# Hybrid encoder layer: norm weights as rows, three squares on GpSimd, and another order of loads and sums in the first stage

## The chip, the cores and the metric

The kernel runs on one core of one Trainium2 chip. The metric is device time in microseconds (us) of one execution. A kernel is run several times, and its median is given. Engines: PE is TensorE, PEld its weight loads, DVE is VectorE, ACT is ScalarE, POOL is GpSimd, SP is SyncE, which here issues transfers (DMA).

## The reference

One layer on 1024 tokens of 1024 values, in float32. The change touches only the beginning of the first feed-forward block:

```
def rms_norm(x, g):
    y = x * rsqrt(mean(x * x, axis=-1) + 1e-6)
    return y * g

h = h + 0.5 * (silu(u @ w_gate) * (u @ w_up)) @ w_down      # u = rms_norm(h, ffn1_norm), D_FF = 2816
u = rms_norm(h, mix_norm); z = u @ w_in                     # then two attention branches
h = h + (sigmoid(ga) * (ya @ w_branch_a) + sigmoid(gb) * (yb @ w_branch_b)) @ w_out
h = h + 0.5 * (silu(v @ w_gate2) * (v @ w_up2)) @ w_down2   # v = rms_norm(h, ffn2_norm)
return rms_norm(h, final_norm)
```

## The kernel before, in words

**Float32 from three products.** Every float32 operand is split in two: a high half, rounded to fp32r by ACT (a copy, or `Copy` with a scale), and a low half, the difference, by DVE (L308 and L311 for weights, L810 and L812 for X, L831 and L833 for blocks of the normed input). A product of a 128-row chunk is three matmuls with 512 columns: high by high (L145), high by low (L147), low by high (L149).

**Seven products.** `hidden` and `products` (L233) compute gate and up projections in two-by-two blocks by a Strassen-like scheme with seven products P1 to P7 for each pair of output tiles i; "P2.1.0" in the tables is product P2 of pair 1, half 0 (gate; half 1 is up). Each has four chunks of three matmuls and one "mm" in the table issues one chunk.

**The input.** The host gives x twice: as rows of tokens (`x`, read into `toks`), and transposed (`xt`): 512 tokens by 128 features a tile. The tiles x:0 to x:3 hold the first half of the tokens: x:2 and x:3 (n = 1) are the features 512 to 1023, chunks X.0 to X.3 (X.0 and X.1 lie in x:2, X.2 and X.3 in x:3), and x:0 and x:1 (n = 0) the others. One norm factor is needed for each token, a sum over all features, so over all four tiles.

**The first stage** (`first_stage`, L734) is written out by hand, under a schedule that keeps the order as written on each engine. `LOADS` (L690) is the order of SP's transfers: x:t the transposed tiles, w:i.m weights of pair i, half m (512 KB; "w:0.1.1" is a part of 256 KB of it), k:t tiles of tokens, h:m second halves of weights. `load_early` (L274) and `fetch` (L284) issue the weights. `TABLE` (L694) is the order of all other work; each token is replayed by `do` (L774) on its own engine:

- `hi:X.c`, `lo:X.c`: halves of x times the norm weight (a scalar for each partition from the tile n1c), without the factor of the token. The P2 products use them raw: the factor is multiplied in afterwards.
- `square:n.c` (L777, ACT): the squares of one 128 x 512 chunk, scaled by 1/D. `add:k` (L780, DVE): sums of two such tiles, six in all; add:1 needs squares 1.0 and 1.1, add:2 square 1.2, add:3 square 1.3, add:4 square 0.0, and so on.
- `sum:0`, `sum:1` (L786, PE): each is four matmuls with the tile of squares as the weights and a column of ones, which gives four columns of means, tokens on partitions. `eps` (L790, DVE), `pow` (L793, POOL): the power -0.5. `spread` (L798, PE): four transposes that lay the factors out along the free axis on all partitions, in a PSUM bank. `keep` (L805, ACT): a copy of it into SBUF. `stat:t` (L801, ACT): sums of squares of the second half's tokens, from `toks`.
- `y:nh.c` (L817, DVE): x times weight times factor, in place; y:11 (n = 0) reads the factor in PSUM, behind `keep` in the order, y:21 (n = 1) reads the copy. `hi`/`lo:B11.c`: its halves, the right operand of the P1 products.
- `hi`/`lo:P2.0.0` and the like: halves of the weights. `mm`, `x`: one chunk of a product; the work behind a finished product.

Ahead of the table, the norm weights come as 128 partitions of 8 values by a transfer on ACT's queue (L739), an ACT instruction with `Silu` (L740) has its table loaded early, and `keep_busy(28)` (L727) runs 28 transposes of the identity on PE, so that it is at work while the first transfers are under way.

Behind the first stage `products.run` takes over, under the same queues; everything from there on is the same in both kernels.

## Time and profile before

| | before |
|---|---|
| runs | 1934.52, 1935.5, 1937.35 us; median 1935.5 us |
| profiled execution, span from first to last instruction | 1934.8 us (its time has no other record than this span) |
| ACT busy | 943.6 us, 49% of the span |
| POOL busy | 295.5 us, 15% |
| DMA, whole span | 298.70 MB, mean 154 GB/s |
| stretch 20 to 22 us: PE busy, granted clock, DMA | 2.00 of 2.00 us, 1.00, 408 GB/s |
| stretch 22 to 24 us: DVE busy | 2.00 of 2.00 us |

The profile is of one execution. Busy time is that of an engine's instructions; matmuls overlap, so a busy PE is not one at its peak, and the distance between the starts of matmuls says more. In a row of the timeline stand the start, the duration, the engine, the line, the operation with output and inputs, and in brackets how long the engine had been idle and what ended it. "SPq" and "ACTq" rows are the issue of a transfer, not the transfer.

### The profile page before, as it was taken

To read this page: it belongs to the slowest core of one execution; us is meant where nothing else is said; L and a number is where in the kernel's file an instruction comes from. 1 tells how busy PE (TensorE), PEld (TensorE's weight loads), DVE (VectorE), ACT (ScalarE), POOL (GpSimd) and SP (SyncE) were. 2 spreads that over 40 slices of the span, in tenths; PEclk is the share of its full clock that TensorE was granted. 3 is DMA by queue.
4 is the path that set the end of the run, shared out by engine and by line. 5 is a ranking of instruction groups with operands and counts; after the bars stand their busy time and mean duration, and the time that the engine had idled before them with its cause. 6 is when DMAs were issued, how large, how long until landed. Compare 5 with 4: busy or idle time off the path is not lost.

```text
span 1934.8 us, 25499 instructions
## 1 busy us (share of the span) xinstructions
PE 1922.2 (99%) x8956; PEld 1603.1 (83%) x8956; DVE 1437.1 (74%) x2560; ACT 943.6 (49%) x1827; POOL 295.5 (15%) x432
## 2 busy tenths in 40 slices
PE   9999999999999999999999999999999999999998
PEld 7888888888888888888888888878888888888886
DVE  7987765668957788678888857889676566569864
ACT  6532333344446543477877862365333333344453
POOL 0011110013300112211122231010111001005210
PEclk9999999999999999999999999999999999999999
DMA  6344323286234478553458576533423323493341
GB/s 261 100 167 163 129 104 128 86 289 225 88 109 137 159 223 250 185 163 104 116 134 195 184 242 210 169 140 133 147 87 109 126 87 109 140 355 104 112 144 61
DMA packets 151745, 298.70 MB, mean 154 GB/s; under 512 B 14912, under 2 KB 64448, under 8 KB 151616
## 3 DMA queue, kind: packets, MB, share of 16 engines
q1 hardware_dynamic: 123072, 210.53, 33.6%
q0 software_dynamic: 27824, 85.48, 13.3%
q8 instruction: 71, 1.16, 0.3%
q10 hardware_dynamic: 720, 1.05, 0.1%
q14 instruction: 58, 0.48, 0.1%
HBM read 210.50 MB, written 88.27 MB: 154 GB/s over the span
## 4 chain that ended last, share of the span: by engine, by line
PE 88%; issue 7%; POOL 1%; DMA 1%; DVE 1%; ACT 1%; POOLq 0%; SPq 0%; ACTq 0%; DVEq 0%
PE g L149 16%; PE g L147 16%; PE g L145 16%; PE d L149 11%; PE d L147 11%; PE d L145 11%; PE d L1299 2%; PE g L1313 1%; PE g L1318 1%; PE d L1278 1%; PE d L1279 1%; POOL zs_d L889 1%; PE d L138 1%; POOL z_d L891 1%; DMA zr_d<-xs 0%
## 5 line engine op out<-in xcount | busy, mean ns | idle before, releaser
L145 PE MATMUL g<-ar,ws 128*128 128x512 f32 x1128 | 423.1, 395 | 0.6 <-ACT fa L911 0.6
L147 PE MATMUL g<-ar,ws 128*128 128x512 f32 x1128 | 417.2, 390 | 0.9 <-DVE ar L94 0.5
L149 PE MATMUL g<-ar,ws 128*128 128x512 f32 x1128 | 416.1, 390 | 0.2 <-DVE ws L311 0.2
L145 PE MATMUL d<-ar,ws 128*128 128x512 f32 x736 | 282.4, 391 | 0.3 <-ACT ar L810 0.2
L147 PE MATMUL d<-ar,ws 128*128 128x512 f32 x736 | 281.9, 390 | 0.3 <-DVE ar L812 0.3
L149 PE MATMUL d<-ar,ws 128*128 128x512 f32 x736 | 281.6, 390 | 0.5 <-DVE ws L311 0.5
L147 PEld LDWEIGHTS g<-ar,ws 128*128 128x128 f32 x1128 | 211.8, 188 | 46.2 <-DVE ar L94 1.0
L149 PEld LDWEIGHTS g<-ar,ws 128*128 128x128 f32 x1128 | 211.7, 188 | 45.5 <-DVE ws L311 0.7
L145 PEld LDWEIGHTS g<-ar,ws 128*128 128x128 f32 x1128 | 206.4, 188 | 37.8 <-ACT fa L911 1.0
L311 DVE TENSOR_TENSOR ws<-raw,ws 128x512 fp32r<-128x512 f32 x204 | 139.6, 690 | 99.6 <-ACT ws L308 98.8
L308 ACT CAST ws<-raw 128x512 fp32r<-128x512 f32 x204 | 125.1, 620 | 140.6 <-PE g L149 64.4
L145 PEld LDWEIGHTS d<-ar,ws 128*128 128x128 f32 x736 | 138.3, 188 | 29.7 <-ACT ar L810 0.6
L147 PEld LDWEIGHTS d<-ar,ws 128*128 128x128 f32 x736 | 138.4, 188 | 29.6 <-DVE ar L812 0.6
L149 PEld LDWEIGHTS d<-ar,ws 128*128 128x128 f32 x736 | 138.4, 188 | 29.4 <-DVE ws L311 0.7
L93 ACT CAST ws<-raw 128x512 fp32r<-128x512 f32 (+1 forms) x121 | 81.0, 669 | 144.0 <-PE d L149 61.8
L94 DVE TENSOR_TENSOR ws<-raw,ws 128x512 fp32r<-128x512 f32 (+1 forms) x119 | 93.7, 789 | 59.8 <-ACT ws L93 59.3
L414 POOL DMA_DIRECT2D hid<-fx x91 | 49.3, 542 | 431.5 <-DVE fx L474 304.9
L93 ACT CAST ar<-raw 128x512 fp32r<-128x512 f32 (+1 forms) x83 | 56.0, 679 | 94.8 <-PE g L147 55.0
L94 DVE TENSOR_TENSOR ws<-ar,ws 128x512 fp32r<-128x512 f32 x114 | 98.3, 867 | 3.8 <-ACT ws L93 3.7
L145 PE MATMUL g<-ws,ws 128*128 128x512 f32 x232 | 91.0, 392 | 0.0
L149 PE MATMUL g<-ws,ws 128*128 128x512 f32 x232 | 90.5, 390 | 0.0
L147 PE MATMUL g<-ws,ws 128*128 128x512 f32 x232 | 90.3, 389 | 0.0
(313 smaller groups left out, 3607.4 us busy)
## 6 DMA issues: line engine op xcount, KB each, us to landing
raw<-hid SPq DMA_DIRECT2D x70, 512.0 KB
hid<-fx POOLq DMA_DIRECT2D x91, 256.0 KB, 2.4
ar<-in_ffn_w_down_dram SPq DMA_DIRECT2D x32, 512.0 KB
raw<-in_ffn_w_up_dram SPq DMA_DIRECT2D x31, 512.0 KB
raw<-in_ffn_w_gate_dram SPq DMA_DIRECT2D x27, 512.0 KB
raw<-in_w_in_dram SPq DMA_DIRECT2D x27, 512.0 KB
hid<-fa POOLq DMA_DIRECT2D x51, 256.0 KB, 2.7
ar<-zs_d POOLq DMA_DIRECT2D x48, 256.0 KB, 5.3
```

The source lines that it names most:

```text
L93: nc.scalar.copy(dst_hi, src)
L94: (eng or nc.vector).tensor_tensor(dst_lo, src, f32v(dst_hi), op=ALU.subtract)
L138: nc.tensor.transpose(pt[:, c * P:(c + 1) * P], xs[:, (half * 4 + c) * P:(half * 4 + c + 1) * P], ident)
L145: nc.tensor.matmul(b, lhs[0], r[0], start=first, stop=False, **kw)
L147: nc.tensor.matmul(b, lhs[0], r[1], start=False, stop=False, **kw)
L149: nc.tensor.matmul(b, lhs[1], r[0], start=False, stop=last, **kw)
L308: nc.scalar.copy(w[0][:, :512], a)
L311: nc.vector.tensor_tensor(w[0][:, 512:], a, f32v(w[0][:, :512]), op=ALU.subtract)
L414: nc.gpsimd.dma_start(hid[PRODUCTS.index(p), i], src)
L889: nc.gpsimd.dma_start(d[ch * P:(ch + 1) * P, cols], t)
L891: nc.gpsimd.dma_start(z_d[ch * P:(ch + 1) * P, cols], c)
L1299: nc.tensor.transpose(pt[:, i * P:(i + 1) * P], un["pr"][s][:, i * P:(i + 1) * P], ident)
```

## The change

- **Norm weights:** eight rows of 128 values, into a corner of the tile that also holds the ones. PE turns them (a transpose with eight rows), DVE copies the result to n1c. Of the 28 transposes of `keep_busy` 6 stay ahead of it and 10 behind. The `Silu` that loads ACT's table works on a corner of another small tile, which is set again afterwards.
- **Squares:** 1.2, 1.3 and 0.0 are a multiplication of the chunk by itself on GpSimd; the other five stay on ACT. The scale 1/D moves to `eps`.
- **Sums:** the column of ones is now 128 columns, so that each matmul of `sum` gives 128 equal columns, four of them a whole PSUM bank; `eps` reads one column of each.
- **Transfers:** w:1.0 and w:1.1 in two parts each, with the parts for P2 (w:1.0.1, w:1.1.1) early; w:0.1.1 ahead of x:3; w:0.0.0 and w:0.1.0 ahead of k:4. SP issues two more transfers.
- **Order:** P2.0.0 and P2.0.1 take turns on X.0 and X.1 before X.2 is used; three chunks of P2.1.0 stand ahead of the sums, its last and the first of P2.1.1 between the sums and the spread; y:11.0 stands right behind the spread, and `keep` comes later, behind all of y:11; halves of B11 alternate with y:11.

```diff
--- before.py
+++ after.py
@@ -275,7 +275,7 @@
 
             if i:
                 ahead[i, m] = r
-                fetch(r, i, m, 0)
+                fetch(r, i, m, 0, slice(0, NC8) if part is None else slice(4 * part, 4 * part + 4))
             else:
                 if (0, m, 0) not in raws:
                     raws[0, m, 0] = raw_slot()
@@ -688,16 +688,18 @@
 
 
     LOADS = """
-        x:2.0 w:0.0.1 x:2.1 x:3 w:0.1.1 x:0 x:1 w:1.0 k:4 w:0.0.0 w:1.1 k:6 w:0.1.0 x:5 k:7 k:5 x:4 x:6 w:2.1 w:2.0
+        x:2.0 w:0.0.1 x:2.1 w:0.1.1 x:3 w:1.0.1 x:0 x:1 w:1.1.1 w:0.0.0 w:0.1.0 k:4 w:1.0.0 w:1.1.0 k:6 x:5 k:7 k:5 x:4 x:6
+        w:2.1 w:2.0
         h:0 h:1 w:3.0 x:7 w:3.1 w:4.1 w:4.0
     """
     TABLE = """
-        hi:X.0 hi:P2.0.0 lo:X.0 square:1.0 lo:P2.0.0 hi:X.1 mm:P2.0.0 square:1.1 lo:X.1 hi:X.2 add:1 mm:P2.0.0 hi:X.3
-        lo:X.2 hi:P2.0.1 lo:X.3 mm:P2.0.0 square:1.2 lo:P2.0.1 square:1.3 mm:P2.0.0 add:2 square:0.0 mm:P2.0.1
-        square:0.1 add:3 mm:P2.0.1 square:0.2 add:4 mm:P2.0.1 square:0.3 add:5 mm:P2.0.1 hi:P2.1.0 add:6 sum:0
-        hi:P1.1.0 lo:P2.1.0 sum:1 stat:4 lo:P1.1.0 mm:P2.1.0 eps:0 hi:P1.0.0 pow:0 mm:P2.1.0 lo:P1.0.0 mm:P2.1.0
-        hi:P2.1.1 hi:P1.1.1 spread:0 lo:P2.1.1 mm:P2.1.0 keep:0 y:11.0 mm:P2.1.1 stat:6 y:11.1 mm:P2.1.1 y:11.2
-        hi:B11.0 mm:P2.1.1 y:11.3 hi:P1.0.1 mm:P2.1.1 lo:B11.0 hi:B11.1 hi:B11.2 lo:P1.0.1 mm:P1.0.0 hi:B11.3 lo:B11.1
+        hi:X.0 hi:P2.0.0 lo:X.0 lo:P2.0.0 hi:X.1 mm:P2.0.0 square:1.0 lo:X.1 hi:P2.0.1 mm:P2.0.0 square:1.1 lo:P2.0.1 hi:X.2
+        mm:P2.0.1 add:1 mm:P2.0.1 lo:X.2 hi:X.3 mm:P2.0.0 lo:X.3 square:1.2 mm:P2.0.1 square:1.3 add:2 mm:P2.0.0
+        hi:P2.1.0 add:3 mm:P2.0.1 square:0.0 lo:P2.1.0 square:0.1 add:4 mm:P2.1.0 square:0.2 add:5 mm:P2.1.0
+        square:0.3 mm:P2.1.0 add:6 sum:0 hi:P2.1.1 hi:P1.0.0 sum:1 lo:P2.1.1 hi:P1.0.1 lo:P1.0.0 eps:0 stat:4 pow:0
+        mm:P2.1.0 lo:P1.0.1 mm:P2.1.1 spread:0 hi:P1.1.0 y:11.0 mm:P2.1.1 y:11.1 hi:B11.0 mm:P2.1.1
+        lo:B11.0 hi:B11.1 mm:P2.1.1 y:11.2 lo:B11.1 hi:P1.1.1 y:11.3 lo:P1.1.0 hi:B11.2 stat:6
+        mm:P1.0.0 hi:B11.3 keep:0
         mm:P1.0.1 stat:7 lo:B11.2 mm:P1.0.0 lo:B11.3 mm:P1.0.1 stat:5 lo:P1.1.1 mm:P1.0.0 x:P2.0.1 mm:P1.0.1 x:P2.1.0
         mm:P1.0.0 y:21.2 mm:P1.0.1 y:21.3 hi:B21.2 mm:P1.1.0 y:21.0 hi:B21.3 mm:P1.1.0 lo:B21.2 hi:B21.0 mm:P1.1.0
         eps:1 hi:P1.2.1 lo:B21.0 pow:1 mm:P1.1.0 hi:P2.2.1 lo:P1.2.1 hi:P1.2.0 mm:P1.1.1 lo:P2.2.1 hi:P2.2.0 mm:P1.1.1
@@ -734,11 +736,12 @@
     def first_stage():
         load, _, _, _, pieces, (multiply, finish), hand_over, load_early = hg
         n1c = const.tile([P, NC8], F32, name="n1c")
-        ones = const.tile([P, 1], F32, name="ones")
+        ones = const.tile([P, 1152], F32, tag="gain", bufs=1, name="ones")
+        ones, n1r = ones[:, :P], ones[:NC8, P:2 * P]
         nc.gpsimd.memset(ones, 1.0)
-        nc.scalar.dma_start(n1c, n1)
-        nc.scalar.activation(ones, ones, AF.Silu)
-        nc.gpsimd.memset(ones, 1.0)
+        nc.scalar.dma_start(n1r, n1)
+        nc.scalar.activation(nhalf4[:, 3:4], nhalf4[:, 3:4], AF.Silu)
+        nc.gpsimd.memset(nhalf4, -0.5)
 
         toks, early = new_ar(4, F32), [new_ar(g, F32) for g in (5, 6)]
         for token in LOADS.split():
@@ -754,7 +757,7 @@
                 load(0, t, 1, 2 + t)
             else:
                 k = 2 * (t - 1) + a[1]
-                load_early(t, a[1], early[k // 4][:, k % 4] if t else None, a[-1])
+                load_early(t, a[1], early[k // 4][:, k % 4] if t else None, a[2] if len(a) > 2 else None)
         room = [xs4(), xs4()]
         sq = [room[k // 2][:, k % 2 * 512:k % 2 * 512 + 512] for k in range(4)]
 
@@ -774,7 +777,11 @@
         def do(op, a):
             if op == "square":
                 n, c = int(a[0]), int(a[1])
-                nc.scalar.activation(sq[place[4 * (1 - n) + c]], block(c, 0, n), AF.Square, scale=D ** -0.5)
+                q, b = sq[place[4 * (1 - n) + c]], block(c, 0, n)
+                if a[0] + a[1] in ("12", "13", "00"):
+                    nc.gpsimd.tensor_tensor(q, b, b, op=ALU.mult)
+                else:
+                    nc.scalar.activation(q, b, AF.Square)
             elif op == "add":
                 d, e = [sq[k] for k in sums[int(a[0])]]
                 nc.vector.tensor_tensor(d, d, e, op=ALU.add)
@@ -783,11 +790,12 @@
                 if i == 0:
                     mean.append(bank("g"))
                 for k in range(4):
-                    nc.tensor.matmul(mean[0][:, k:k + 1], sq[3 * i][:, k * P:(k + 1) * P], ones, start=i + k == 0, stop=i == 1,
-                                     skip_group_check=True)
+                    nc.tensor.matmul(mean[0][:, k * P:(k + 1) * P], sq[3 * i][:, k * P:(k + 1) * P], ones, start=i + k == 0,
+                                     stop=i == 1, skip_group_check=True)
             elif op == "eps":
                 i = int(a[0])
-                nc.vector.tensor_scalar(st[i][1], st[1][0] if i else mean[0][:, :4], EPS, None, op0=ALU.add)
+                ms = st[1][0] if i else mean[0].rearrange("p (k f) -> p k f", f=P)[:, :, 0]
+                nc.vector.tensor_scalar(st[i][1], ms, 1.0 if i else 1.0 / D, EPS, op0=ALU.mult, op1=ALU.add)
             elif op == "pow":
                 i = int(a[0])
                 nc.gpsimd.tensor_tensor(st[i][0], st[i][1], nhalf4, op=ALU.pow)
@@ -847,7 +855,11 @@
                         pc[q] = pieces(*q)
                     pc[q].pop(op)()
 
-        keep_busy(28)
+        keep_busy(6)
+        pt = bank("g")
+        nc.tensor.transpose(pt[:, :NC8], n1r, ident[:NC8, :NC8])
+        nc.vector.tensor_copy(n1c, pt[:, :NC8])
+        keep_busy(10)
         for token in TABLE.split():
             op, a = token.split(":")
             do(op, a.split("."))
@@ -1536,7 +1548,7 @@
     first, second = data["x"].reshape(2, 512, D)
     data["xt"] = np.concatenate([first.reshape(512, 2, 2, 2, P).transpose(1, 2, 4, 3, 0).reshape(4, P, D),
                                  second.reshape(512, 2, 4, P).transpose(2, 3, 1, 0).reshape(4, P, D)])
-    data["ffn1_norm"] = data["ffn1_norm"].reshape(NC8, P).T
+    data["ffn1_norm"] = data["ffn1_norm"].reshape(NC8, P)
     for name in ("ffn1_w_gate", "ffn1_w_up", "ffn2_w_gate", "ffn2_w_up"):
         data[name] = data[name].reshape(NC8, P, NF, P).transpose(2, 1, 0, 3)
     data = {name: data[name] for name in _INS}
```

## The prediction

> **What bounds the kernel now.** I read the page first: busy shares and the chain that ended last.
>
> ```profile
> span 1934.8 us, 25499 instructions
> ...
> PE 1922.2 (99%) x8956; PEld 1603.1 (83%) x8956; DVE 1437.1 (74%) x2560; ACT 943.6 (49%) x1827; POOL 295.5 (15%) x432
> ...
> PE 88%; issue 7%; POOL 1%; DMA 1%; DVE 1%; ACT 1%; POOLq 0%; SPq 0%; ACTq 0%; DVEq 0%
> ```
>
> TensorE bounds the kernel from end to end: 1922.2 of 1934.8 us, so it is idle for 12.6 us in all. The diff touches only the first 30 us. Built, the two programs differ in their first 79 (before) and 68 (after) PE instructions and agree in the 8870 behind them; the last 2527 on DVE, 1639 on ACT, 424 on POOL and 488 on SP agree in order too. So the question is how much earlier or later PE leaves the first stage; what it gains there it keeps as long as the later transfers allow.
>
> Next the timeline of the first 30 us. Columns: start, duration, engine, line, operation, and in brackets the idle time before it and what ended that. Here PE is not simply busy.
>
> ```profile
> 0.73 0.40 ACTq L739 DMA_DIRECT2D n1c<-in_ffn_norm_dram  x1
> ...
> 1.38 5.38 PE L732 MATMUL g<-ident 128*128 128x128 f32 x28 [1.38 <-POOL ident masks.py:199]
> ...
> 3.90 0.72 ACT L810 ACTIVATE ar<-fx,n1c 128x512 fp32r<-128x512 f32 x1 [1.24 <-DMA n1c<-in_ffn_norm_dram]
> ...
> 4.62 0.62 ACT L308 CAST ws<-raw 128x512 fp32r<-128x512 f32 x1
> ...
> 6.52 0.48 PE L145 MATMUL d<-ar,ws 128*128 128x512 f32 x1
> ...
> 7.57 0.33 SPq L752 DMA_DIRECT2D ar<-in_x_dram  x1
> ...
> 7.58 1.34 ACT L810 ACTIVATE ar<-fx,n1c 128x512 fp32r<-128x512 f32 x2 [0.68 <-DMA fx<-in_xt_dram]
> ...
> 7.76 0.40 PE L149 MATMUL d<-ar,ws 128*128 128x512 f32 x1
> ...
> 8.36 0.51 PE L145 MATMUL d<-ar,ws 128*128 128x512 f32 x1 [0.19 <-ACT ar L810]
> 8.57 0.33 SPq L285 DMA_DIRECT2D raw<-in_ffn_w_up_dram  x1
> ...
> 9.14 0.50 PE L147 MATMUL d<-ar,ws 128*128 128x512 f32 x1 [0.28 <-DVE ar L812]
> ...
> 10.40 0.39 PE L145 MATMUL d<-ar,ws 128*128 128x512 f32 x1
> ...
> 10.62 0.40 PE L147 MATMUL d<-ar,ws 128*128 128x512 f32 x1
> ...
> 12.90 0.39 PE L149 MATMUL d<-ar,ws 128*128 128x512 f32 x1
> ...
> 13.49 1.92 PE L786 MATMUL g<-ones,xs 128*128 128x1 f32 x16 [0.20 <-DVE xs L780]
> ...
> 15.27 0.48 PE L145 MATMUL d<-ar,ws 128*128 128x512 f32 x1
> ...
> 15.45 0.16 DVE L790 TENSOR_SCALAR st<-g 128x4 f32<-128x4 f32 x1 [0.29 <-PE g L786]
> ...
> 16.09 0.63 PE L145 MATMUL d<-ar,ws 128*128 128x512 f32 x1
> ...
> 18.65 0.96 PE L798 MATMUL g<-ident,st 128*128 128x128 f32 x4
> ...
> 19.36 0.48 PE L145 MATMUL d<-ar,ws 128*128 128x512 f32 x1
> ...
> 22.90 0.39 PE L145 MATMUL g<-ar,ws 128*128 128x512 f32 x1
> ...
> 23.65 0.50 PE L147 MATMUL g<-ar,ws 128*128 128x512 f32 x1 [0.36 <-DVE ar L833]
> ```
>
> The same timeline, PE alone, at the end of the stage:
>
> ```profile
> 29.00 0.39 PE L145 MATMUL g<-ar,ws 128*128 128x512 f32 x1
> ...
> 31.72 0.39 PE L145 MATMUL g<-ar,ws 128*128 128x512 f32 x1
> ```
>
> Twelve matmuls lie between 29.00 and 31.72, so one is issued each 0.227 us. From 6.52 to 29.00 there are 72 of them (six products of four chunks of three), 16.36 us at that pace in 22.48 us: **6.12 us are lost**. Where: before X.2 the starts are 7.76, 8.36, 9.14, and the three gaps about them cost 1.0; the sums lie between 12.90 and 15.27 and cost 2.14 (2.37 less 0.23); six matmuls from 16.09 to 18.65 take 2.56 instead of 1.36, 1.2 lost; the spread, 18.65 to 19.36, costs 0.7; the wait for B11's low half, 22.90 to 23.65, costs 0.6 with its restart. That is 5.7; some 0.4 I cannot place.
>
> The table by stretches says what the slow matmuls are (columns: busy time of PE, PEld, DVE, ACT, POOL; granted clock; DMA share; GB/s):
>
> ```profile
> 16.00:18.00 2.00, 2.00 (x6) 1.53 (x6) 1.13 (x2) 0.87 (x2) 0.79 (x1) 0.50 1.03 402
> ...
> 12.56:15.98 3.42, 3.22 (x23) 2.70 (x22) 2.81 (x6) 3.40 (x7) 0.22 (x1) 1.00 1.04 412
> ...
> 5.74:9.15 3.41, 2.94 (x17) 2.00 (x15) 2.44 (x5) 2.73 (x6) 0.00 (x0) 1.00 1.00 351
> ```
>
> From 16 us the granted clock is 0.50, just behind the stretch with 1.92 us of one-column sums. DMA is at its full share of 1.0, 402 to 412 GB/s: order of transfers is a matter of who waits, not of volume.
>
> **The change, part by part.** *Norm weights and warm-up.* Before, the high half of X.0 waited for n1c until 3.90 and the first weight half was cast by 5.24, but PE came out of its 28 transposes only at 6.52. After, 6 transposes, the turn of n1, a DVE copy (0.16 by L790's row) and 10 more. Twenty-eight took 5.38, 0.19 each, so 17 take 3.3 and end near 4.9 unless n1 is late. When eight rows land no row shows; the bounds are the end of their issue (1.1) and as late as before (3.9). Up to some 3.4 the weight half, cast by 5.24 as now, is the later one, and the first matmul comes at 5.3; at 3.9 eleven transposes follow, 0.2 each, and it comes at 6.2. I take 5.3, as fewer and longer rows should not be slower than many short ones: 1.2 earlier.
>
> *Order of transfers and of the first matmuls.* Both P2 products now take X.0 and X.1 first: twelve matmuls, 5.3 to 8.03 (9.0 at the late bound). But x:3 goes behind w:0.1.1. SP's issues at 7.57 and 8.57 each follow the landing of an older transfer, of x:3 and of w:0.1.1 as I read them; exchanged, x:3 lands at 8.57, 1.0 later. The high half of X.2 is then there at 9.3 and the 13th matmul starts at 9.36, against 10.40 before: 1.0 ahead, whatever the start was. PE has waited 1.33 for it, so the earlier first matmul is worth nothing by itself. The halves of w:1.0 and w:1.1 that P2.1 needs come some 3 us earlier; the two extra SP issues cost 0.33 each on a queue that waits anyway. Nothing there.
>
> *Three squares on GpSimd.* ACT is rid of three squares of 0.6 us. What they do to DVE is the disputed price. Far from here, GpSimd and DVE work side by side on such tiles (timeline of POOL and of DVE, then the groups of POOL):
>
> ```profile
> 454.91 6.69 POOL L563 TENSOR_TENSOR ar<-ar,ar 128x512 f32<-128x512 f32 x4 [19.72 <-DMA ar<-in_ffn_w_down_dram]
> ```
> ```profile
> 454.64 0.69 DVE L94 TENSOR_TENSOR ws<-raw,ws 128x512 fp32r<-128x512 f32 x1 [0.93 <-ACT ws L93]
> 455.25 1.78 DVE L94 TENSOR_TENSOR ws<-ar,ws 128x512 fp32r<-128x512 f32 x1
> 457.07 1.68 DVE L560 TENSOR_TENSOR ar<-ar,ar 128x512 f32<-128x512 f32 x1
> ```
> ```profile
> L94 POOL TENSOR_TENSOR ws<-raw,ws 128x512 fp32r<-128x512 f32 x2 | 2.5, 1292 | 14.6 <-ACT ws L93 14.6
> ```
>
> DVE's two-input operation takes 0.69 alone and 1.68 to 1.78 beside GpSimd, whose own takes 1.67 (6.69 for four) instead of 1.29: they take turns. Applied here: the first square starts with x:3 at 8.6 and ends at 9.85; X.2's low half on DVE (9.36) waits for it and ends at 10.40 instead of 10.1, so the 14th matmul starts at 10.44 (before 10.62). X.3's low half ends at 11.06; the second square, which had its turn in between, at 11.56; add:2 at 12.1; the third square at 13.3; add:3 at 13.8; and the low half of P2.1.0, queued behind add:3, at 14.44. PE has done 24 matmuls by 13.0 and stands before the third of P2.1.0 from 13.45 to 14.48: a new hole of 1.1 with its restart. Without turns that half is ready at 12.9 and there is no hole.
>
> *Sums with 128 columns.* PE instructions stay 16. The bounds are 0.1 each (as now) and 0.23 (a 512-column matmul, or a cold transpose): 1.7 to 3.6. The nearest row is the 128-column transposes of the same type, 0.19 mostly cold and half of it warm; I take 1.8 in all, with no wait, as P2.1.0 covers the adds: 0.35 less than before. The cold stretch behind them, 1.2, should go, since the array streams 128 columns where it had one.
>
> *The rest.* 1/D in the eps operation costs nothing (same instruction). Spread after the first chunk of P2.1.1: 0.44 warm and 0.15 of wait for the power, against 0.7. The y of B11 no longer stand behind the copy; B11's first low half comes 1.3 earlier, but PE is there earlier too and waits 0.65 in two places, as before.
>
> **Sum**, to the 73rd matmul: 5.3 + 16.36 + 1.33 + 0.86 (X.2's halves) + 1.1 + 1.8 + 0.6 + 0.65 = 28.0; with 0.3 for what I could not place, 28.3, against 29.00. That is **0.7 us earlier**, at most 0 if a later transfer holds PE. The profiled execution's span is 1934.8 and the runs have a median of 1935.5 (1934.52 to 1937.35); from between the two, 1935.1, less 0.7: 1934.4.
>
> **Rivals.** *Squares ride free.* If a square (one tile read twice) does not make DVE take turns, the 1.1 hole and 0.3 at X.2 go: 28.3 less 1.4, 2.1 us gained, about 1933.0. For it: no row has a GpSimd operation with one input twice. Against: in the rows above every such pair of operations took turns.
>
> *Slower: PE's clock drops in the new holes.* It decides at the granted clock from 16 us on. The stretch before that has a hole of 1.1 of 3.4 us; if it drops the clock as the one-column sums did, 16 sum instructions at 0.21 instead of 0.11 cost 1.7, within a slow stretch as long as before's (16.09 to 19.36). The end is 28.3 + 1.7 = 30.0, 1.0 later than before: 1936.1. For it: before, the clock fell behind a stretch whose PE idle time was 0.2 us, with less than half of it in 512-column matmuls. Against: behind 5.74 to 9.15, with 0.47 idle, it stayed at 1.00. The Trainium skill, "TensorE: Matmul & The Clock Gate", Part 1 (What's actually happening), says that the clock halves only after a whole idle window of about 3.4 us; by that rule this rival costs nothing. The trace does not bear it out: the 0.50 at 16 us follows no idle window.
>
> *It doesn't do what it says.* The x:3 wait eats the front and the rest is even: PE leaves where it left, 1935.1; this lies inside the forecast's own spread.
>
> **How the numbers follow.** The forecast with its even variant 0.55 (1933.7 to 1935.8), squares free 0.22, clock drop 0.17, unforeseen 0.06. The runs of before alone spread over 2.8 us, so I widen both ends: from 1931.9 (squares free, 1.1 below) to 1937.2 (clock drop and a high median). A measurement of this kernel tells about 0.2%, 3.9 us, from no change: faster than 1931.6 needs squares free and more, 0.11; slower than 1939.4 needs a cold clock in two stretches, 0.08; within 0.81.
>
> **What would show it.** In the changed kernel: first matmul near 5.3; 13th at 9.4 behind X.2; squares on POOL of 1.2 to 1.7 us with DVE's low halves and adds stretched to 1.1 to 1.7; a hole of 1 us in P2.1.0 at 13.5 to 14.5; granted clock 1.00 from 16 to 20; 73rd matmul near 28.3. Wrong if DVE's operations beside the squares take 0.7, if the clock is 0.50 anywhere behind 6 us, or if x:3 lands before 8.

## The result, and the profile after

The changed kernel has a median of 1939.28 us (13 runs, 1936.99 to 1942.19) against 1936.07 of the kernel before (13 runs, 1934.52 to 1938.03): a ratio of 1.0015 [1.0008, 1.0022], so it is **slower by 0.15%**, some 3 us. Forecast were 0.7 us gained and 1931.9 to 1937.2: the sign is wrong, and the time lies outside the range. The difference is less than the 0.2% that I took for what a measurement can tell; thirteen runs of each tell more. The execution profiled took 1939.36 us. First its page, the rows that answer to those of before.

```profile
span 1937.3 us, 25481 instructions
...
PE 1922.6 (99%) x8945; PEld 1601.0 (83%) x8945; DVE 1438.7 (74%) x2561; ACT 942.6 (49%) x1824; POOL 299.4 (15%) x435
...
q8 instruction: 70, 1.15, 0.2%
...
PE 87%; issue 8%; POOL 2%; DVE 1%; DMA 1%; ACT 1%; SPq 0%; POOLq 0%; ACTq 0%; DVEq 0%
```

PE is as busy as before (1922.6 us against 1922.2), but the span is 2.5 us longer: it is idle for more. Next the first 30 us of the changed kernel, all engines (start, duration, engine, line, operation, idle time before and what ended it), and PE alone at the end of the stage.

```profile
2.96 0.27 PE L860 MATMUL g<-ident,ones 8*128 8x8 f32 x1
...
5.45 0.80 PE L145 MATMUL d<-ar,ws 128*128 128x512 f32 x1
...
7.68 0.80 PE L145 MATMUL d<-ar,ws 128*128 128x512 f32 x1 [0.58 <-ACT ar L818]
...
9.41 1.33 ACT L818 ACTIVATE ar<-fx,n1c 128x512 fp32r<-128x512 f32 x2 [0.16 <-DMA fx<-in_xt_dram]
9.46 4.38 POOL L782 TENSOR_TENSOR xs<-fx 128x512 f32<-128x512 f32 x3 [6.46 <-DMA fx<-in_xt_dram]
9.48 0.63 PE L145 MATMUL d<-ar,ws 128*128 128x512 f32 x1
...
9.91 0.63 PE L147 MATMUL d<-ar,ws 128*128 128x512 f32 x1
...
10.17 2.77 DVE L820 SCALAR_TENSOR_TENSOR ar<-fx,n1c,ar 128x512 fp32r<-128x512 f32 x2
...
11.62 0.39 PE L145 MATMUL d<-ar,ws 128*128 128x512 f32 x1
...
12.86 2.32 DVE L787 TENSOR_TENSOR xs<-xs,xs 128x512 f32<-128x512 f32 x2
...
15.10 0.68 DVE L311 TENSOR_TENSOR ws<-ar,ws 128x512 fp32r<-128x512 f32 x1
...
15.84 0.50 PE L149 MATMUL d<-ar,ws 128*128 128x512 f32 x1 [0.86 <-DVE ws L311]
```
```profile
17.58 1.95 PE L793 MATMUL g<-ones,xs 128*128 128x128 f32 x16
19.28 0.48 PE L145 MATMUL d<-ar,ws 128*128 128x512 f32 x1
...
20.52 0.40 PE L149 MATMUL d<-ar,ws 128*128 128x512 f32 x1
21.27 0.65 PE L806 MATMUL g<-ident,st 128*128 128x128 f32 x4 [0.35 <-POOL st L801]
21.68 0.48 PE L145 MATMUL d<-ar,ws 128*128 128x512 f32 x1
...
29.91 0.39 PE L145 MATMUL g<-ar,ws 128*128 128x512 f32 x1
```

Three things are to be seen. The first matmul comes at 5.45, but up to 10.8 two matmuls are 0.43 apart (9.48, 9.91), not 0.23: PE runs at half speed. The three squares on POOL (4.38) stand beside two low halves on DVE (2.77) and two adds (2.32); behind them PE waits before 15.84 for the low half of P2.1.0. This chain on DVE begins behind X.2's high half, which ACT could start only when x:3 had landed, at 9.41; from 10.17 to 15.78 DVE has no pause. The sums take 1.70 (17.58 to 19.28), with no slow matmul behind them. The 73rd matmul starts at 29.91 instead of 29.00.

So the stage accounts for 0.9 us of the 2.5 by which the span grew. The other 1.6 lie **behind** it, where the forecast had nothing. Set beside those of before in order, the starts of PE's instructions show two places where it loses over half a microsecond. Here they are in the timeline of the changed kernel (PE, then all engines).

```profile
972.24 0.44 PE L1311 MATMUL d<-ident,fa 128*128 128x128 f32 x2 [0.34 <-DVE ws L94]
```
```profile
1088.25 2.39 POOL L94 TENSOR_TENSOR ar<-raw,ar 128x1024 fp32r<-128x1024 f32 x1 [1.76 <-ACT ar L93]
...
1088.28 2.78 DVE L1085 TENSOR_TENSOR fa<-raw,masks 128x384 f32<-128x384 f32 x1
...
1091.45 0.44 PE L1290 MATMUL d<-ar,ar 128*128 128x384 f32 x1 [1.08 <-DVE nmx L1295]
```

At 971 PE loses 0.74 us, at 1090 1.4; small gains and losses elsewhere come to −0.5. The diff touches neither place.

### The profile page after: what moved, and what is told of

The parts are those of the page before. It is cut to its first block, busy times and chain, and to the rows that moved or that the text cites. A ratio compares the mean times of both kernels' runs of the same rounds, so it can differ in the third digit from the quotient of the medians.

```text
span 1937.3 us, 25481 instructions
## 1 busy us (share of the span) xinstructions
PE 1922.6 (99%) x8945; PEld 1601.0 (83%) x8945; DVE 1438.7 (74%) x2561; ACT 942.6 (49%) x1824; POOL 299.4 (15%) x435
## 3 DMA queue, kind: packets, MB, share of 16 engines
q8 instruction: 70, 1.15, 0.2%
q10 hardware_dynamic: 592, 1.05, 0.1%
## 4 chain that ended last, share of the span: by engine, by line
PE 87%; issue 8%; POOL 2%; DVE 1%; DMA 1%; ACT 1%; SPq 0%; POOLq 0%; ACTq 0%; DVEq 0%
PE g L149 16%; PE g L147 16%; PE g L145 16%; PE d L149 11%; PE d L147 11%; PE d L145 11%; PE d L1311 2%; PE g L1330 1%; PE d L1290 1%; PE d L1291 1%; PE g L1325 1%; POOL zs_d L901 1%; PE d L138 1%; POOL z_d L903 1%; DMA fx<-in_xt_dram 0%
## 5 line engine op out<-in xcount | busy, mean ns | idle before, releaser
L145 PE MATMUL g<-ws,ws 128*128 128x512 f32 x232 | 91.0, 392 | 0.0
L1298 ACT ACTIVATE fa<-fa,nmx 128x385 f32<-128x385 f32 (+3 forms) x128 | 75.7, 592 | 31.1 <-DVE nmx L1295 30.3
L149 PE MATMUL g<-ws,ws 128*128 128x512 f32 x232 | 90.4, 390 | 0.0
```

The costliest lines, as they stand in the source:

```text
L145: nc.tensor.matmul(b, lhs[0], r[0], start=first, stop=False, **kw)
L149: nc.tensor.matmul(b, lhs[1], r[0], start=False, stop=last, **kw)
L1298: nc.scalar.activation(pr, pr, AF.Exp, scale=-1.0, bias=nmx[:, s:s + 1], accum_out=ssum[:, s:s + 1])
```

## The experiments

All runs in one table. "73rd" is the start of the 73rd matmul in the profiled execution; "behind" is what is left of the span from there, against the 1905.8 us (1934.8 less 29.00) of the kernel before in its first trace. Times are medians of 11 runs (13 in the first row), beside those of the kernel before measured together with them; ratios have 95% intervals. before_2, before_3 and after_2 are single executions. A profiled execution need not be typical: those of a_sq_act (1934.56) and b_16 (1935.34) are the fastest of their eleven.

| run | us | before | ratio | 73rd | behind |
|---|---|---|---|---|---|
| changed kernel | 1939.28 | 1936.07 | 1.0015 [1.0008, 1.0022] | 29.91 | +1.6 |
| after_2 (again) | 1942.11 | 1935.85 | | 29.11 | +5.4 |
| before_2, before_3 | 1935.61, 1935.63 | 1935.85 | | 28.99, 28.73 | −1.0, −0.6 |
| a_sq_act | 1937.22 | 1936.14 | 1.0006 [0.9997, 1.0015] | 27.15 | −0.2 |
| a_warm | 1937.28 | 1936.14 | 1.0005 [0.9996, 1.0014] | 28.62 | +1.1 |
| a_warm_sq | 1936.56 | 1935.89 | 1.0004 [0.9995, 1.0013] | 27.93 | −0.1 |
| a_late_spread | 1936.68 | 1935.85 | 1.0003 [0.9994, 1.0012] | 27.48 | +1.6 |
| a_loads_old | 1938.98 | 1936.14 | 1.0014 [1.0005, 1.0023] | 30.96 | +1.2 |
| a_sum1 | 1938.46 | 1936.14 | 1.0012 [1.0003, 1.0020] | 29.55 | +2.3 |
| a_pad | 1938.45 | 1936.42 | 1.0007 [0.9998, 1.0016] | 29.81 | +0.9 |
| a_sq_pad | 1937.58 | 1936.42 | 1.0004 [0.9995, 1.0013] | 28.85 | +1.8 |
| b_sq_pool | 1939.08 | 1935.89 | 1.0016 [1.0007, 1.0025] | 31.19 | −1.2 |
| b_front | 1937.18 | 1935.89 | 1.0006 [0.9997, 1.0015] | 27.76 | +1.4 |
| b_16 | 1937.84 | 1936.42 | 1.0008 [0.9999, 1.0017] | 27.70 | +0.1 |
| b_sum128 | 1935.44 | 1935.89 | 0.9999 [0.9990, 1.0008] | 27.56 | +0.1 |
| b_sum128_2 | 1936.35 | 1936.42 | 0.9999 [0.9991, 1.0008] | 27.99 | +0.8 |

A median's interval is about ±1.7 us wide, as wide as most of the steps. So the stage is read from the traces, and the medians only bear out the sum.

**Squares.** a_sq_act is the changed kernel with all squares on ACT; b_sq_pool is the kernel before with the three squares on GpSimd.

```diff
-                if a[0] + a[1] in ("12", "13", "00"):
+                if a[0] + a[1] in ():
```

> The changed kernel with all eight squares on ACT again; everything else as changed. Theory A (GpSimd's squares hold DVE up): in the changed kernel the low halves of X.2 and X.3 took 2.77 us for two and the low half of P2.1.0 was ready only at 15.8; without GpSimd's squares it is ready by 14.4, the hole before the 27th matmul (14.59 to 15.84) goes, and the first stage ends 1.0 us earlier than in the changed kernel (73rd matmul at 28.9 instead of 29.91). Theory B (the cold clock and the late transfers at the front are the loss): the 27th matmul moves by under 0.3 us and the stage ends where it did, 29.9. Theory C (what is lost is lost behind the first stage): the stage may gain, but the time stays near 1939.

In b_sq_pool the same branch, with 1/D moved to `eps`, is put into the kernel before:

```diff
-                nc.scalar.activation(sq[place[4 * (1 - n) + c]], block(c, 0, n), AF.Square, scale=D ** -0.5)
+                q, b = sq[place[4 * (1 - n) + c]], block(c, 0, n)
+                if a[0] + a[1] in ("12", "13", "00"):
+                    nc.gpsimd.tensor_tensor(q, b, b, op=ALU.mult)
+                else:
+                    nc.scalar.activation(q, b, AF.Square)
```

> The kernel before with one part of the change: squares 1.2, 1.3 and 0.0 on GpSimd. Theory A (GpSimd's squares hold DVE up): the two low halves of X.2 and X.3 take over 2 us instead of 1.41, the second operand of X.2 comes at 9.7 or later instead of 9.14, the sums start 0.5 to 1.5 us later than 13.49, and the stage ends 0.5 to 1.5 us later than 29.0. Rival (the squares ride free): DVE's times as before, stage end within 0.3 us.

Timelines of a_sq_act, and of after_2 (the changed kernel, in a trace in which x:3 landed at the same time as there), each with the 27th matmul as its last row:

```profile
8.61 1.34 ACT L818 ACTIVATE ar<-fx,n1c 128x512 fp32r<-128x512 f32 x2 [0.53 <-DMA fx<-in_xt_dram]
...
9.37 1.41 DVE L820 SCALAR_TENSOR_TENSOR ar<-fx,n1c,ar 128x512 fp32r<-128x512 f32 x2 [0.50 <-ACT ar L818]
...
10.70 1.48 DVE L787 TENSOR_TENSOR xs<-xs,xs 128x512 f32<-128x512 f32 x2
...
12.10 0.69 DVE L311 TENSOR_TENSOR ws<-ar,ws 128x512 fp32r<-128x512 f32 x1
...
13.24 0.39 PE L149 MATMUL d<-ar,ws 128*128 128x512 f32 x1
```
```profile
8.70 4.37 POOL L782 TENSOR_TENSOR xs<-fx 128x512 f32<-128x512 f32 x3 [5.70 <-DMA fx<-in_xt_dram]
...
9.40 2.77 DVE L820 SCALAR_TENSOR_TENSOR ar<-fx,n1c,ar 128x512 fp32r<-128x512 f32 x2
...
12.09 2.32 DVE L787 TENSOR_TENSOR xs<-xs,xs 128x512 f32<-128x512 f32 x2
...
14.33 0.69 DVE L311 TENSOR_TENSOR ws<-ar,ws 128x512 fp32r<-128x512 f32 x1
...
15.07 0.50 PE L149 MATMUL d<-ar,ws 128*128 128x512 f32 x1 [0.97 <-DVE ws L311]
```

Beside the squares DVE's two low halves take 2.77 instead of 1.41 and its two adds 2.32 instead of 1.48. The half of P2.1.0 is begun 2.23 later, and the 27th matmul 1.83 later; without the squares on GpSimd PE has no hole there. The 73rd is at 29.11 against 27.15, 1.96 apart; in the median the squares on ACT are worth 0.0009 (1.0015 less 1.0006). In b_sq_pool the same lines show 2.97 for the two low halves, and PE pays at once:

```profile
7.71 4.16 POOL L779 TENSOR_TENSOR xs<-fx 128x512 f32<-128x512 f32 x3 [4.89 <-DMA fx<-in_xt_dram]
...
9.45 2.97 DVE L816 SCALAR_TENSOR_TENSOR ar<-fx,n1c,ar 128x512 fp32r<-128x512 f32 x2
...
11.03 0.50 PE L147 MATMUL d<-ar,ws 128*128 128x512 f32 x1 [1.92 <-DVE ar L816]
```

It leaves the stage at 31.19, 2.2 later than before (0.5 to 1.5 were expected), and is 0.16% slower by itself. Behind that hole of 1.92 its clock is 0.50 from 12.32 to 15.73: what the forecast's slower rival saw coming in the changed kernel happened here. (The kernel before has such a stretch too, behind its sums.) That the squares hold DVE, and that PE pays about 2 us for it, is shown from both sides.

**Front.** a_warm has 22 transposes behind the turn instead of 10, so 28 in all as before; b_front puts only the eight rows, their turn and 6 + 10 transposes into the kernel before.

```diff
-        keep_busy(10)
+        keep_busy(22)
```

> The changed kernel with 22 instead of 10 transposes behind the turn of the norm weights, so that PE is busy without a gap until about 7.5 us. Theory B (cold clock at the front): no matmul is issued 0.43 apart, the 13th comes at 10.5 instead of 11.62, and the stage ends about 1 us earlier. Theory A (DVE beside GpSimd is what ends last): the 13th matmul comes earlier too, but the 27th still waits for the low half of P2.1.0 until 15.8, and the stage ends at 29.9 as before; time within 0.3 us of the changed kernel.

> The kernel before with one part of the change: norm weights as eight rows turned by PE, and 6 + turn + 10 transposes for 28. Theory B (fewer transposes leave PE's clock cold): matmuls 0.43 apart in part of 5.5 to 11 us; the waits at X.2 (8.4 and 9.1) hide the first of it, so the first stage ends 0 to 1.3 us later than before (73rd matmul at 29.0 to 30.3), and the median is above that of before. Rival (the front is hidden behind X.2 whatever the clock): 73rd matmul within 0.3 us of 29.0.

In a_warm the first matmul comes at 6.43, later than 5.45, but matmuls are 0.23 apart from it on wherever PE does not wait; the 27th starts at 14.57 instead of 15.84 and the 73rd at 28.62. That looks like the gain of a warm clock. Its rows say otherwise:

```profile
8.51 1.34 ACT L818 ACTIVATE ar<-fx,n1c 128x512 fp32r<-128x512 f32 x2 [0.53 <-DMA fx<-in_xt_dram]
...
9.27 2.40 DVE L820 SCALAR_TENSOR_TENSOR ar<-fx,n1c,ar 128x512 fp32r<-128x512 f32 x2 [0.50 <-ACT ar L818]
...
14.57 0.50 PE L149 MATMUL d<-ar,ws 128*128 128x512 f32 x1 [0.97 <-DVE ws L311]
```

PE waits 0.97 for the low half of P2.1.0 here too, so DVE ends last, not the clock. Of the 1.27 by which the 27th is earlier, 0.90 come from x:3, which landed earlier in this execution (X.2's high half begins at 8.51 instead of 9.41), and 0.37 from the two low halves (2.40 instead of 2.77). From the start of that high half to the 73rd matmul it is 20.11 us here against 20.50 and 20.46 in the two traces of the changed kernel; with the squares on ACT it is 18.54 with 16 transposes (a_sq_act) and 18.56 with 28 (a_warm_sq). So the cold start is real, and it costs this stage little or nothing.

Of the nine traces with 16 transposes ahead of the first matmul, seven show 0.43 spacing at its start (till 11.1 in the changed kernel, 7.7 in b_front, 10.4 in b_16); of the nine with 28, none does. In part the matmuls behind 28 just start later, at 6.40 to 7.47 instead of 5.25 to 6.10. The column of granted clocks doesn't show this: for 8 to 10 us of the changed kernel it says 1.00 with five matmuls in 2 us. The trace's first record of the clock is at 11.09 there; ahead of it the column just reads 1.00.

```profile
8.00:10.00 2.00, 2.00 (x5) 1.25 (x5) 1.66 (x3) 1.84 (x4) 0.54 (x1) 1.00 1.05 425
...
18.00:20.00 2.00, 2.00 (x17) 1.91 (x16) 1.42 (x4) 2.00 (x5) 0.13 (x1) 1.00 1.04 416
```

b_front leaves the stage at 27.76, 1.2 ahead of the first trace of before: about what the half clock behind the sums costs there, which b_front doesn't show. The gain is lost again behind the stage (+1.4), and the median is 1.0006. Neither expectation for the end of the stage came true.

**Order of transfers.** a_loads_old is the changed kernel with the list `LOADS` of before.

> The changed kernel with the transfers in the order of the kernel before (x:3 ahead of w:0.1.1, w:1.0 and w:1.1 whole). If the order of transfers made x:2.1 and x:3 late (6.9 and 9.4 us in the changed kernel, 5.3 and 7.6 before), they land at 5.3 and 7.6 again, the high half of X.2 is ready at 8.3, but the P2.0.1 chunks wait for w:0.1.1 until about 10 and P2.1.0 for w:1.0 until 13.8: the stage ends between 28.9 and 30.4. If something else at the front made them late (the load of eight rows), they land at 6.9 and over 8.5 here too.

The 73rd is at 30.96, 1.05 later than in the first trace of the changed kernel and beyond the expected 30.4. x:3 is there at 8.2, but w:0.1.1 only at 9.05; PE has holes ahead of that, and the clock is 0.50 from 8.22 to 15.05. P2.1.0 waits for w:1.0 until 13.0, but PE comes to it only at 16.57, so this costs nothing here. By this one trace the new order of transfers is worth about a microsecond inside this order of work; the time, 1.0014, doesn't tell it from the changed kernel.

**Sums.** a_sum1 is the changed kernel with one-column sums (`ones[:, :1]`, one column of the bank each); b_sum128 and its repeat b_sum128_2 are the kernel before with sums of 128 columns.

> The changed kernel with one column of ones in the sums instead of 128. If the wide sums keep PE's clock up, it drops to 0.50 for 3.4 us behind the sums here, as before, and the stage ends 1 to 1.5 us later than in the changed kernel (73rd matmul at 31). If the clock is set by the holes and the grid of its windows rather than by the sums, the stage ends within 0.3 us of 29.9.

> The kernel before with one part of the change: 128 columns of ones in the sums. If the one-column sums had dropped the clock, it stays at 1.00 from 16 us on, and the stage ends 1.2 to 1.5 us earlier than 29.0 in every execution. If the clock falls by other holes (X.2, the wait for the sums) and by where its 3.4 us windows happen to lie, the sums' width changes nothing and the median is within 0.5 us of that of before.

> The kernel before with 128 columns in the sums, once more, for a second trace and another series of times. In the first, PE's clock stayed at 1.00 and the stage ended 1.44 us earlier than before, with a median of 1935.44 against 1935.89. If the half clock behind one-column sums is the rule (three of three traces of before) and the wide sums prevent it, it is absent again, the 73rd matmul comes at 27.3 to 27.8, and the median is 0.3 to 1.5 us under that of before.

The sums take the same time with either width (1.84 to 2.02 by their rows). In each of the three traces of before the clock is 0.50 for 3.4 us behind them; in b_sum128 and b_sum128_2 it stays at 1.00, and the 73rd comes at 27.56 and 27.99, 0.7 to 1.4 earlier than in those three. Their medians, 0.45 and 0.07 under the kernel before, hardly show it. But the clock stays at 1.00 with one column too, in a_sum1, b_front, b_16 and b_sq_pool; a_sum1 ends the stage at 29.55, near the 29.9 and far from the 31 of its two expectations. The stretch from 18 to 20 us of before_2, b_sum128_2 and b_16 (busy PE, PEld, DVE, ACT, POOL; granted clock):

```profile
18.00:20.00 2.00, 2.00 (x8) 1.60 (x8) 0.00 (x0) 0.34 (x1) 0.00 (x0) 0.50 1.01 404
```
```profile
18.00:20.00 2.00, 2.00 (x12) 1.73 (x11) 0.77 (x2) 1.39 (x2) 0.00 (x0) 1.00 1.03 412
```
```profile
18.00:20.00 2.00, 2.00 (x12) 1.65 (x11) 1.06 (x2) 1.68 (x4) 0.00 (x0) 1.00 1.03 412
```

So 128 columns may keep the clock up, yet the width alone isn't what decides: that the one-column sums drop it, as I put it, fell. Something else goes with it. Inside the stage the clock's records in the traces last 3.41, 6.83 or 10.24 us, all multiples of 3.41, so the time can be cut into stretches of 3.41 at their borders. The stretch with all sixteen one-column sums holds the starts of 5, 6 and 6 matmuls of 512 columns in the three traces of before, and 0.50 follows; it holds 7 in b_16, a_sum1 and b_sq_pool, and 1.00 stays. (In b_front a border divides the sums.) With sums of 128 columns 5 are enough, in b_sum128. This is the stretch of b_16, where PE is never idle; that of before is 12.56:15.98 in the prediction, with PE idle for 0.20:

```profile
13.76:17.18 3.42, 3.42 (x24) 3.14 (x24) 2.89 (x6) 3.24 (x7) 1.17 (x1) 1.00 1.03 406
```

No run varied that count alone, so it is a reading of these traces, not shown; what decides stays open.

**Chance.** The two kernels once more, unchanged.

> The kernel before, unchanged, profiled a second time. If the stretch of half clock behind its sums (16 to 19.4 us, 1.2 to 1.5 us lost) belongs to the kernel, it is here again and the 73rd matmul comes at 29.0 within 0.3. If it hangs on where the clock's 3.4 us windows lie in an execution, it may be missing, and the stage then ends near 27.6; a difference of up to 2 us may then also arise behind the stage.

> The kernel before, unchanged, profiled a third time: as for the second. Should all three show the half clock at 16 us, the stretch belongs to the kernel; if one or two do, it is chance of the execution.

> The changed kernel, unchanged, profiled a second time. By the runs so far x:3 lands between 8.5 and 9.4 and the clock at the front is cold until between 5 and 11 us, by chance; the hole before the 27th matmul must be there again (1.0 to 1.3 us), the low halves of X.2 and X.3 take over 2.3 us for two, and the stage ends between 28.6 and 30.2.

after_2 was warm from its first matmul and left the stage 0.8 earlier than the first trace of the changed kernel, then lost 5.4 behind it: 2.3 in a wait at 750, 1.7 in a half-clock stretch at 753, 0.74 at 971, and smaller ones. So "behind" moves by several us from one execution to the next; only what comes back in every trace of a kind can be put down to a change.

**Both mends, and the spread.** a_warm_sq has both edits above; a_late_spread is the same with the spread one chunk later (`mm:P2.1.1 mm:P2.1.1 spread:0`, one `mm:P2.1.1` fewer behind).

> The changed kernel with both suspected costs taken out: all squares on ACT, and 22 transposes behind the turn. Theories A and B together: no hole before the 27th matmul and no cold matmul at the front; the 73rd matmul at 27.0 (1.9 earlier than before), and a median 1 to 2 us under the kernel before. Theory C (something behind the first stage costs 1.5 us in the changed kernel): the stage ends at 27.0, but the median is not below that of before.

> The changed kernel with all squares on ACT, 22 transposes behind the turn, and the spread one chunk later (behind two chunks of P2.1.1 instead of one). In the same kernel with the spread where the change put it, PE waited 0.38 us for the power and lost 0.8 there. If PE can use that chunk, the 73rd matmul comes 0.3 to 0.8 us earlier (27.1 to 27.6 instead of 27.9) and the median is 0 to 1 us under the kernel before. If the blocks of B11 then come later by as much, the stage ends at 27.9 again.

PE's wait for the power before the spread is gone in a_late_spread, but 0.5 of it comes back as a wait for B11's low half: 27.48 against 27.93. Even this difference is not the spread's. ACT begins X.2's high half in a_warm_sq and in a_late_spread:

```profile
9.37 1.34 ACT L818 ACTIVATE ar<-fx,n1c 128x512 fp32r<-128x512 f32 x2
```
```profile
8.74 1.34 ACT L818 ACTIVATE ar<-fx,n1c 128x512 fp32r<-128x512 f32 x2 [0.64 <-DMA fx<-in_xt_dram]
```

From there to the 73rd matmul it is 18.56 and 18.74, so the later spread gained nothing; and a_warm_sq misses the expected 27.0 because it starts there 0.76 later than a_sq_act. Both leave the stage over 1 us before the first trace of before, and both medians, 1.0004 and 1.0003, still don't beat the kernel before.

**Behind the stage.** So a gain in the stage doesn't reach the median. One loss behind it that comes back is that at 971, although these two kernels, with 28 transposes, don't have it. It begins at 963, with a copy on ACT. ACT alone in that stretch, in the kernel before, the changed kernel, b_16 and a_pad, which follow below:

```profile
962.97 1.07 ACT L1127 COPY xs<-g 128x512 f32<-128x512 f32 x2 [0.46 <-PE g L149]
```
```profile
964.49 1.07 ACT L1139 COPY xs<-g 128x512 f32<-128x512 f32 x2 [1.63 <-PE d L1311]
```
```profile
962.51 1.07 ACT L1127 COPY xs<-g 128x512 f32<-128x512 f32 x2 [1.60 <-PE d L1299]
```
```profile
963.40 1.07 ACT L1142 COPY xs<-g 128x512 f32<-128x512 f32 x2 [0.39 <-PE g L149]
```

The copy is begun 1.2 us late in the changed kernel, and PE stands at 972 for what follows from it. In the three us up to the end of ACT's instruction ahead of that copy, the view of DMA queues shows this in the changed kernel and in b_16:

```profile
q8 instruction: 1, 0.02, 2.3%
```
```profile
q8 instruction: 1, 0.02, 2.3%
```

Found to half a microsecond, it lies at 961.5 to 962.0 in the changed kernel, 0.9 to 1.4 ahead of the end of that instruction, and as far ahead in b_16. In the same three us of before and a_pad there is none; there it lies 7.5 to 8.0 ahead (at 954.5 to 955.0 in before). Queue q8 brings code in blocks of 16 KB (1.15 MB in 70, by the page). By the pages it brings 70 blocks in the seven traces with 16 transposes and none put back, and 71 in the eleven others, so their number goes with PE's instructions. The changed kernel has 12 transposes fewer on PE (and the one turn more), and if q8 is PE's own code, each of its later blocks is due that much later in the program. Two kernels test that alone: b_16 takes 12 transposes out of the kernel before, and a_pad puts 12 back into the changed kernel, in its hole ahead of P2.1.0; a_sq_pad is a_pad with the squares on ACT.

```diff
-        keep_busy(28)
+        keep_busy(16)
```

> The kernel before with 16 transposes instead of 28 and nothing else changed. Code theory: the fetch moves to 1.2 us ahead of ACT's copy at 963 us, ACT's wait there is 1.5 to 1.7 us instead of 0.46, PE loses 0.7 to 0.95 at 971; median 0.5 to 2 us above that of before although the first stage ends at 27.7 to 29.3 as before. Chance theory: no loss at 971, median within 0.5 us of before.

```diff
-        ... square:0.1 add:4 mm:P2.1.0 square:0.2 ...
+        ... square:0.1 add:4 busy:12 mm:P2.1.0 square:0.2 ...
```

> The changed kernel with 12 more transposes of the identity, put ahead of the first chunk of P2.1.0, where PE waits about 1 us for the low half of P2.1.0 anyway; the front stays as changed (6, the turn, 10). Code theory (12 fewer PE instructions at the front move every later fetch of PE's code; with 16 transposes a fetch meets an ACT instruction at 963 us that then comes 1.2 us late and costs PE 0.7 to 0.95 at 971): the fetch lies 7.7 us ahead of that place as in the kernels with 28, ACT's wait there is 0.4 to 0.5 us instead of 1.5 to 1.7, and the loss at 971 is gone; median 1 to 2 us under the changed kernel's 1939.3. Chance theory: the loss at 971 appears or not regardless, and the median stays at 1939.3 or above.

> The changed kernel with all squares on ACT, the front as changed (6, the turn, 10), and 12 transposes ahead of the first chunk of P2.1.0, where here PE does not wait, so that they cost up to 1.3 us. Code theory: no loss at 971 (it was there with the same squares and 16 transposes); first stage at 28 to 28.6; median 0 to 1 us under the 1937.2 of the kernel without the 12, despite the later stage. Front theory (the cold start is what 22 transposes cured): the median is not below 1937.2.

b_16 has the late copy and loses 0.74 at 971; a_pad and a_sq_pad have neither. Over all traces: seven of seven with 16 transposes and none put back lose it, none of the other eleven does. That the count of PE's instructions decides this loss is shown. That the block delays ACT is argued from its place alone; a block of 8 KB on q14, which I take for ACT's own code, begins 0.4 to 0.8 behind the end of q8's in these seven, and the copy starts 0.4 to 0.8 behind the end of that. Which of the two holds ACT stays open. The medians bear the loss out only in part: b_16 is 1.4 above the kernel before, as expected; a_pad is 0.8 under the changed kernel, where 1 to 2 were expected; a_sq_pad, expected to be up to 1 under the 1937.2 of a_sq_act, is 0.4 above it, with a stage that ends 1.7 later.

The loss at 1090 is of another kind. The same place in after_2, where it did not occur:

```profile
1092.71 0.55 DVE L1085 TENSOR_TENSOR fa<-raw,masks 128x384 f32<-128x384 f32 x1
...
1092.91 2.61 POOL L94 TENSOR_TENSOR ar<-raw,ar 128x1024 fp32r<-128x1024 f32 x1 [1.98 <-ACT ar L93]
```

There DVE's operation of 128x384 has started 0.20 ahead of POOL's and takes 0.55. In the changed kernel POOL started at 1088.25, 0.03 ahead of it, and it takes 2.78; PE waits 1.08 for what follows. The Trainium skill, "SBUF — State Buffer", section "SBUF: two separate sides", says that a DVE operation with two inputs in SBUF and a GpSimd operation that reads SBUF share one pair of ports, and that whoever starts first holds it for the whole instruction: these two traces agree, 0.55 or 2.78 by who came first. DVE waited in this way in 5 of 10 traces of kernels made from the changed one (among them a_pad and a_sq_pad), where POOL's row starts 0.024 or more ahead of DVE's, and in none of 8 made from the kernel before. There POOL is ahead in three, by 0.017 at most, and DVE takes 0.55 all the same; four of the eight lie within 0.02 of a tie. So it is not shown that the change moves this race. What sets the two a few tenths apart so far behind the stage was not found.

## Why the prediction was wrong

The profiled execution lies 4.96 us above the forecast, 1939.36 against 1934.4. Three terms make that up: 1.76 in the base (2.06 between time and span, where I had 0.3), 1.61 in the stage (29.91 less 28.3), 1.59 behind it (2.5 less 0.91). By the medians of thirteen runs it is 0.97 in the base (1936.07 against 1935.1) and 3.9 in the change (3.2 lost instead of 0.7 gained).

- **The base** ("from between the two, 1935.1"). I set the time beside a span of 1934.8 as if the two were almost one. In each run that has both, the time is 1.7 to 2.1 above the span (1939.36 and 1937.3 here; 1935.61 and 1933.8 in before_2), so an execution with that span takes 1936.5 to 1936.9. Three runs were also too few: with thirteen the median of before is 1936.07.
- **Front** ("the first matmul comes at 5.3"; "the earlier first matmul is worth nothing by itself"). It came at 5.45. But I took 0.23 a matmul from then on. With 16 transposes PE is mostly still cold when it starts, so in the first trace the 13th matmul started at 11.62, not 9.36; x:3, landed by 9.41, was by then no longer what it waited for. In after_2, warm, it was at 9.76, and a_sq_act's 13th at 9.45. The pace was wrong, and the row of before was there to see it by: 28 transposes in 5.38, "mostly cold". That the start by itself is worth nothing held all the same: the 27th matmul waits for DVE, and the cold clock only shortened that wait.
- **Order of transfers.** x:3 landed at 8.5 to 9.4 in the traces with the new list, against 8.57 forecast: right, at the early edge. In the first trace it is 9.41, and that is 0.8 of the 1.61 in the stage.
- **Squares** ("X.3's low half ends at 11.06; the second square, which had its turn in between"). The mechanism was right, the price too low. After_2, with x:3 as forecast, ends X.3's low half at 12.17: it waits for a square too, as X.2's does. A square takes 1.46, not 1.25 (1.04 where DVE leaves it alone, the first in a_loads_old). Cost at the 27th matmul 1.83 against 1.4; in the first trace of the changed kernel the low half of P2.1.0 is 0.8 late by x:3 and 0.5 more by the turns (the 27th at 15.84 instead of 14.48).
- **Sums** (1.8, no wait): 1.70, no wait, and the clock was 1.00 from 16 to 20. The forecast of that was right, its reason was not shown (b_16, b_front, a_sum1). The rival in which the clock drops in the new hole did not occur here: 18 to 20 us is at 1.00 beside a hole of 1.0. It did in b_sq_pool, behind a hole of 1.92.
- **Spread** (0.44 and 0.15 of wait): 0.93, from 20.52 to 21.68 less 0.23. The power on GpSimd took 1.35, where the row of before has 1.03.
- **Behind the stage** ("what it gains there it keeps as long as the later transfers allow"). This is the step that failed by its reason. The instructions behind the stage do agree, but not their distance from the start of PE's program. At 971 that costs 0.7 in every trace with 11 or 12 PE instructions fewer; the race at 1090 takes 1.4 in half of them. "Later transfers" were named, the transfers of code were not. The account does not close: of the 3.2 us in the medians the stage has 0.1 to 0.9 by the two traces, 971 has 0.74 and the race 0.7 on average, so 0.9 to 1.7 stay without a cause found. Nor was it found why a_warm_sq, a_late_spread, b_sum128 and b_sum128_2, which have no loss at 971 and leave the stage 1.0 to 1.5 before the first trace of before, lie between 0.45 under and 0.83 above the kernel before in the median.

The Trainium skill, "Runtime: NRT & Kernel Launch", section "Instruction fetch mechanics", says that an engine's instructions are streamed in blocks of 16 KiB and that crossing a block's end is mostly hidden. The trace agrees on the block for q8 (1.15 MB in 70); q14 moves 8 KB at a time (0.48 MB in 58). Whether the 0.74 us at 971 are a case that isn't hidden is argued above, not shown.

By the table, squares on ACT give back 0.0009 and the 12 transposes 0.0008 of the 0.0015, and both together 0.0011; the intervals overlap, so these shares are rough.

## What to carry to other kernels

Where a stage of 30 us saves 1 us in a kernel of 1935, look first at whether the gain can arrive: adding or removing instructions also moves the blocks of code behind them, and a race of two engines for SBUF 1000 us later can take back more than was won. Before two traces are compared, see when the transfer landed that both hang on: x:3 alone moved this stage by up to 0.9 from one execution to another. Work shifted from ACT to GpSimd is paid by DVE's two-input operations beside it, one instruction at a time; here each of them took up to 1.52 us instead of 0.69 to 0.75. And set a forecast on the median of many runs, not on a span: here the base alone was off by 1.0 us in the median and 1.8 in the profiled execution, more than the 0.7 that was forecast as gained.

## What the runs showed of the hardware that was not expected

- **Transposes and the clock.** After 16 transposes of 128x128 the first matmuls start 0.43 apart in seven of nine traces; after 28, in none of nine. The granted clock in the profile says 1.00 there before its first record, so only the spacing shows it.
- **A half clock without a cause in sight.** The three traces of before have 3.4 us of 0.50 behind the sums, with PE hardly idle ahead of it (0.2 us); b_16, with the same sums and 12 transposes fewer ahead, has none. The stretch of 3.41 us with the sums holds 5 or 6 other matmuls there and 7 here.
- **One block of code.** A 16 KB block of q8 about 1 us ahead of an ACT copy goes with a start 1.2 us late, and 0.74 us lost on PE 8 us later.
- **A few hundredths decide over 2.2 us.** POOL at 1088.25 and DVE at 1088.28: DVE's operation takes 2.78 instead of 0.55. With POOL 0.017 ahead, in before_3, DVE's takes 0.55.
